# First feed-forward block in two phases with seven products for eight, and the state-space tables moved beside its second layer

## The chip, the cores and the metric

The program runs on one core of one Trainium2 chip. The metric is the device time of one execution in microseconds; before the change it was 2383.15 us, the median of three runs (2380.75 to 2388.32). TensorE multiplies a stationary block of up to 128 x 128 weights with moving columns, VectorE (DVE), ScalarE (ACT) and GpSimd (POOL) work element by element, and the queues of SyncE (SP), ACT and POOL issue DMAs.

## The reference

One layer of a hybrid decoder for 1024 prompt positions and 8 sample positions, 1032 rows of 1024 channels in all:

```
x = x + 0.5 * swiglu(rms_norm(x, g_ffn1), w1_gate, w1_up, w1_down)   # 1024 -> 2816 -> 1024
h = rms_norm(x, g_mix); proj = h @ w_in                              # u | q | k | v | gates
y_ssm  = s5_branch(u, ...)      # state-space model, 32 groups, needs tables from a, dt, b, c
y_attn = dilated attention over three windows
x = x + (gate_ssm * (y_ssm @ w_ssm_proj) + gate_attn * (y_attn @ w_attn_proj)) @ w_o
x = x + 0.5 * swiglu(rms_norm(x, g_ffn2), w2_gate, w2_up, w2_down)
swiglu(x) = (silu(x @ w_gate) * (x @ w_up)) @ w_down
```

It also returns key/value windows (mostly copies of the caches) and the final state-space states.

## The kernel before

The rows of x are transposed to channels on the partitions and split into three chunks of 344 columns (`CH`, `NCH`): `xT[c]` is 128 x 8 x 344. All products run with each operand split into a high and a low part (`ah`/`al` for x, `h`/`l` for weights: a ScalarE cast and a VectorE subtraction, `loadw` and `parts`), and three matmuls stand for one exact product. The hidden width 2816 makes 22 tiles f of 128, or 11 pairs j.

*First block, before* (`ffn`, L171): for each f, `gateup` loads a gate and an up tile (512 KB each), splits them, and makes both products for each of the three chunks, 8 x 3 matmuls each; the hidden values stay in SBUF, split (`hh`, `hl`). After every second f, `down` multiplies the pair before with its rows of `w1_down` and adds into `xT` on VectorE (L200). The last four f are one group, chunk by chunk, and after each chunk `norm` makes the operands of the next stage. `fill` calls `ssm_tables` for one of ten steps per pair: step 0 (`ssm_poles`) is a long chain of small VectorE instructions; the following ones make the state-space tables of four groups each: powers R on GpSimd (L416 to L430, doubling a length from 1 to 128, one buffer R), products on VectorE, transposes on TensorE, stores by SP.

`load_x` (L916) loads x in nine blocks, makes each row's scale by ACT and VectorE, transposes on TensorE and copies into `xT`; after blocks 2, 5 and 8 `scaled` makes the operands of a chunk.

*Second block, before and after*: in two phases. `wo_norm` (L1244) stores the chunk's x to `x_d` (a DMA by POOL), sums squares, scales `xT` in place and makes the operands: chunks 0 and 1 together are a 2 x 2 block matrix (channels halves by chunks), for which seven products stand for eight; their operands B11, B21, B22, T1 to T4 are halves of the chunks, and sums and differences of them; D0 and D1 are chunk 2, done directly. `wprep` makes the weights' sums. `ffn_up` (L1350) runs through f: products A11 B11, S2 T2, S3 T3, S1 T1, A12 B21, A22 T4, S4 B22, then chunk 2's; `second` forms what the second layer needs of the hidden values and stores it to `hs_d` by POOL. `ffn_down` (L1493) runs the pairs j in groups, product by product (P1 to P7 and `lo`, `hi` for chunk 2): `hload` fetches an operand from `hs_d` into one of four slots in turn (the first four by SP, then by POOL), `wsplit` splits the weights, `run` makes four PSUM banks and adds them into accumulators. The operand slots are memory of the first layer's operands (`slot`, `SLOT`).

The order of work: instructions are written in program order, and a planner orders each engine's queue by a simulated timeline: what comes earlier in the program goes first when it is ready, and what is ready may go ahead of what isn't. DMAs follow on the queue that issues them. `keep_in_program_order` holds the cache copies on ACT's queue (one after each weight load, `shift`) and the loads of x (`xin`).

After the first block, `mix` makes u tiles, eight state-space batches that read the tables from memory, gates, attention and the output projection.

Of the kernel before, what the change touches and what calls it, by code (L numbers as in the profile page):

```python
# [12 lines left out]
ALU = mybir.AluOpType  # L13
# [46 lines left out]
class Step:  # L60
# [49 lines left out]
    def norm(s, pool, c, z, xT, ah, al):  # L110
        nc = s.nc
        ss = pool.tile([128, CH], F32, name="ss", bufs=1)
        for k in range(KT):
            if k == 0:
                nc.scalar.activation(ss, xT[c][:, k], AF.Square)
            else:
                sq = pool.tile([128, CH], F32, name="sq", bufs=2)
                nc.scalar.activation(sq, xT[c][:, k], AF.Square)
                (nc.gpsimd if k <= PN[z] else nc.vector).tensor_add(ss, ss, sq)
        p = s.pt.tile([128, 512], F32, name="pT")  # L120
        nc.tensor.matmul(p[:, :CH], s.ones, ss, start=True, stop=True)
        s.scaled(pool, c, z, xT, ah, al, s.rsq(pool, p[:, :CH], 1.0 / D))

    def scaled(s, pool, c, z, xT, ah, al, r):
        nc = s.nc
        for k in range(KT):
            xn = pool.tile([128, CH], F32, name="xn", bufs=2 if z else XN)
            nc.vector.scalar_tensor_tensor(xn, xT[c][:, k], s.gains[:, z, k:k + 1], r, op0=ALU.mult, op1=ALU.mult)  # L128
            nc.scalar.copy(ah[c][:, k], xn)  # L129
            (nc.gpsimd if k % PL[z] == 1 else nc.vector).tensor_sub(al[c][:, k], xn, ah[c][:, k])  # L130

# [33 lines left out]

    def new_act(s):
        s.ah = [s.act.tile([128, KT, CH], F32R, name=f"ah{c}") for c in range(NCH)]
        s.al = [s.act.tile([128, KT, CH], F32R, name=f"al{c}") for c in range(NCH)]


    def ffn(s, hp, tmp, wg, wu, wd, xT, after, fill=None, lg=4):  # L171
        nc = s.nc
        H = {}

        def gateup(f):
            Wg, Wu = s.pre or (s.colw(wg, 128 * f), s.colw(wu, 128 * f))
            s.pre = None
            hh = hp.tile([128, NCH, CH], F32R, name="hh")
            hl = hp.tile([128, NCH, CH], F32R, name="hl")
            for c in range(NCH):  # L180
                pg, pu = s.dense(Wg, c), s.dense(Wu, c)
                h = tmp.tile([128, CH], F32, name="h")
                nc.scalar.activation(h, pg, AF.Silu)
                nc.vector.tensor_mul(h, h, pu)  # L184
                nc.scalar.copy(hh[:, c], h)
                nc.vector.tensor_sub(hl[:, c], h, hh[:, c])
            H[f] = hh, hl

        def down(fs):
            W = [s.loadw(wd[0][128 * f:128 * f + 128, :].rearrange("p (m q) -> p m q", q=128)) for f in fs]  # L190
            last = fs[-1] == NF - 1
            if last:
                order = [(m, c) for c in range(NCH) for m in range(KT)]
            else:
                order = [(m, c) for m in range(KT) for c in range(NCH)]
            for m, c in order:
                p = s.pm.tile([128, 512], F32, name="pm")[:, :CH]
                for i, f in enumerate(fs):
                    s.mm3(p, W[i], H[f], [(m, c)], i == 0, i == len(fs) - 1)
                nc.vector.scalar_tensor_tensor(xT[c][:, m], p, 0.5, xT[c][:, m], op0=ALU.mult, op1=ALU.add)  # L200
                if last:
                    after(c, m)

        for f in range(0, NF, 2):
            gateup(f)
            gateup(f + 1)
            if f and f < NF - 2:
                down((f - 2, f - 1))
            if fill:
                fill(f // 2)  # L210
        if lg < 4:
            down(range(NF - 4, NF - lg))
        down(range(NF - lg, NF))
# [606 lines left out]
    def run(s):  # L820
        tc, nc, i = s.tc, s.nc, s.i
        with ExitStack() as ctx:
# [49 lines left out]

            with ExitStack() as c1:
                psum(c1, 6, 2)
                xp, tmp = pool(c1, "xp"), pool(c1, "tmp", 2)
                xT = [xp.tile([128, KT, CH], F32, name=f"xT{c}") for c in range(NCH)]
                s.new_act()

                def first():
                    s.pre = s.colw(i['w1_gate'], 0), s.colw(i['w1_up'], 0)  # L880

                with ExitStack() as c_:
                    s.load_x(pool(c_, "xrp"), xT, first)
                stp = pool(c1, "stp")
                hp = pool(c1, "hp", 4)

                def after(c, m):
                    if m < KT - 1:
                        return
                    if c == 0:  # L890
                        s.new_act()
                    s.norm(tmp, c, 1, xT, s.ah, s.al)
                    nc.sync.dma_start(s.x_d[c], xT[c])

                s.ffn(hp, tmp, i['w1_gate'], i['w1_up'], i['w1_down'], xT, after, lambda n: s.ssm_tables(stp, tmp, n), LG)
# [3 lines left out]
            with ExitStack() as c6:  # L899
                hp = pool(c6, "hp2")  # L900
                c2, c01 = ExitStack(), ExitStack()
                x2, tmp, x01 = pool(c2, "x2"), pool(c2, "tmp2", 2), pool(c01, "x01")
                xT = [(x2 if c == 2 else x01).tile([128, KT, CH], F32, name=f"xT{c}") for c in range(NCH)]
                s.join(hp, xT)
                s.ep = pool(ctx, "ep", side="right")
                s.wprep(i['w2_gate'], i['w2_up'])
                s.out_norm(tmp, xT)
                c01.close()
                s.ep2 = pool(ctx, "ep2", side="right")
                s.ffn_up(pool, c6, c2, hp)  # L910
            s.wd = [pool(ctx, f"wd{z}", side="right") for z in range(2)]
            s.ffn_down(pool(ctx, "wsum", side="right"), pool(ctx, "yo"), i['w2_down'])
# [3 lines left out]
    def load_x(s, tmp, xT, first):  # L916

        nc = s.nc
        R = {}
        for b in range(9):  # L920
# [3 lines left out]
            if b == 2:  # L924
                first()
# [24 lines left out]
            if b in (2, 5, 8):  # L950
                s.scaled(tmp, b // 3, 0, xT, s.ah, s.al, R[b // 3][:, :CH])
# [33 lines left out]
    def mix(s, psum):  # L985
# [15 lines left out]
        if True:  # L1001
# [132 lines left out]
    def u_tile(s, up, m):  # L1134
        nc = s.nc
        W = s.colw(s.i['w_in'], 128 * m)
        ut, us = up.tile([128, 8, 128], F32, name="ut"), up.tile([128, 8], F32, name="us", bufs=2)
        for ch in range(NCH):
            p = s.dense(W, ch)
            nn = 43 if ch < 2 else 42  # L1140
            nc.scalar.copy(ut[:, :, 43 * ch:43 * ch + nn].rearrange("p j n -> p n j"),
                           p[:, :8 * nn].rearrange("p (n j) -> p n j", j=8))
            if ch == 2:
                nc.scalar.copy(us, p[:, 336:344])
        for g in range(8):
            dst = s.u_d[8 * m + g, 7, 0]
            nc.sync.dma_start(bass.AP(tensor=dst.tensor, offset=dst.offset, ap=[[128, 16], [-2048, 8], [1, 128]]),
                              ut[16 * g:16 * g + 16])
        nc.sync.dma_start(s.us_d[128 * m:128 * m + 128], us)
# [94 lines left out]
    def wo_norm(s, tmp, xT, c):  # L1244
# [4 lines left out]
        ss = tmp.tile([128, CH], F32, name="rs3", bufs=1)  # L1249
        for k in range(KT):  # L1250
            if k == 0:
                nc.scalar.activation(ss, xT[c][:, k], AF.Square)
            else:
                sq = tmp.tile([128, CH], F32, name="sq", bufs=2)
                nc.scalar.activation(sq, xT[c][:, k], AF.Square)
                V.tensor_add(ss, ss, sq)
            if k % 4 == 3:
                yield 1
        p = s.pt.tile([128, 512], F32, name="pT")
        nc.tensor.matmul(p[:, :CH], s.ones, ss, start=True, stop=True)  # L1260
        r = s.rsq(tmp, p[:, :CH], 1.0 / D)
        yield 1
        for k in range(KT):
# [456 lines left out]
```

## Time and profile before

| | us |
|---|---|
| median of 3 runs | 2383.15 |
| profiled execution, its own time | 2386.82 |
| its span on the core | 2384.8 |
| TensorE, VectorE, ScalarE, GpSimd busy | 2306.0, 1356.1, 786.9, 339.4 |
| mean granted TensorE clock | 0.981 |

Stages of the span: loading x to about 36 us, the first block to about 814 us, u tiles and state-space batches to about 1060 us, attention to 1380 us, output projection to about 1660 us, the second block's first layer to 2128.5 us and its second to the end. "Busy" of an engine is the time in which at least one of its instructions ran; idle time of an engine that others don't wait for costs nothing.

### The profile page before, as it was taken

The page shows a single profiled execution, that of the slowest core. Times are in us where ns is not written, and L with a number is a line of the kernel's source. Part 1 is how long each engine was busy: PE and PEld are TensorE (multiplying, and loading weights), DVE is VectorE, ACT ScalarE, POOL GpSimd, SP SyncE. Part 2 cuts the span into 40 slices and gives each one's busy share as a digit, 9 for nine tenths or more (in the row PEclk, how much of TensorE's full clock was granted, in tenths as well). Part 3 has the DMA queues.
Part 4 walks back from the last instruction along what each step waited for, and adds up shares of the span by engine and source line. Part 5 has one row for each costly group of instructions (what it writes and reads, how often), then busy time and mean ns, then how long its engine had stood idle before and what let it go on. Part 6 is the DMA issues. An engine that isn't in the chain of part 4 may idle for free.

```text
span 2384.8 us, 37168 instructions
## 1 busy us (share of the span) xinstructions
PE 2306.0 (97%) x14409; PEld 2212.2 (93%) x14409; DVE 1356.1 (57%) x2929; ACT 786.9 (33%) x1506; POOL 339.4 (14%) x929
## 2 busy tenths in 40 slices
PE   6999999999999899989999998899999999998999
PEld 6999999999999799978888897899999999998998
DVE  7655544364532834456476536488867676644574
ACT  6211112111112434455453523145433333332322
POOL 3056777000000300000000000210001000010010
PEclk8999999999999999999999998999999999998999
DMA  5333334242323377561142135766334333374553
GB/s 142 99 102 115 115 107 136 80 121 86 108 81 113 125 185 235 165 201 45 48 123 66 43 115 153 260 201 210 130 119 140 119 122 124 119 301 188 192 205 125
DMA packets 300198, 325.73 MB, mean 137 GB/s; under 512 B 38822, under 2 KB 265494, under 8 KB 297462
## 3 DMA queue, kind: packets, MB, share of 16 engines
q1 hardware_dynamic: 277478, 189.94, 26.6%
q0 software_dynamic: 18864, 85.21, 10.0%
q10 hardware_dynamic: 3680, 48.22, 6.5%
q8 instruction: 113, 1.85, 0.3%
q14 instruction: 63, 0.52, 0.1%
HBM read 243.52 MB, written 123.78 MB: 154 GB/s over the span
## 4 chain that ended last, share of the span: by engine, by line
PE 77%; DMA 8%; issue 6%; DVE 6%; ACT 2%; SPq 1%; POOL 0%; ACTq 0%; POOLq 0%; DVEq 0%
PE pm L158 44%; PE pm L1347 19%; PE pm L1544 8%; DMA r<-in_w_o_dram 2%; PE ps L671 1%; DMA rs<-g_d 1%; DMA e<-hs_d 1%; PE acc L687 1%; PE pT L680 1%; PE pn L973 1%; DVE w L1242 1%; DVE xn L128 1%; DMA xr<-in_x_prompt_dram 0%; PE pT L457 0%; DMA r<-in_w_in_dram 0%
## 5 line engine op out<-in xcount | busy, mean ns | idle before, releaser
L158 PE MATMUL pm<-ah,w 128*128 128x344 f32 x4192 | 1010.1, 324 | 14.1 <-ACT ah L129 3.8
L158 PEld LDWEIGHTS pm<-ah,w 128*128 128x128 f32 x4192 | 727.8, 189 | 31.5 <-issue 9.5
L158 PE MATMUL pm<-al,w 128*128 128x344 f32 x2384 | 722.5, 326 | 6.2 <-ACT al L1172 2.8
L158 PEld LDWEIGHTS pm<-al,w 128*128 128x128 f32 x2384 | 443.2, 190 | 17.8 <-issue 8.1
L158 PE MATMUL pm<-hh,w 128*128 128x344 f32 x1056 | 253.7, 321 | 0.0
L143 ACT CAST w<-r 128x1024 fp32r<-128x1024 f32 (+1 forms) x124 | 120.5, 978 | 369.6 <-PE pm L158 340.7
L144 DVE TENSOR_TENSOR w<-r,w 128x1024 fp32r<-128x1024 f32 (+1 forms) x124 | 142.3, 1149 | 154.1 <-ACT w L143 141.6
L1241 ACT CAST w<-r 128x1024 fp32r<-128x1024 f32 (+1 forms) x130 | 125.6, 968 | 295.0 <-PE pm L1347 171.5
L158 PEld LDWEIGHTS pm<-hh,w 128*128 128x128 f32 x1056 | 183.6, 188 | 0.4
L1242 DVE TENSOR_TENSOR w<-r,w 128x1024 fp32r<-128x1024 f32 (+1 forms) x130 | 145.3, 1120 | 67.5 <-ACT w L1241 67.4
L1347 PE MATMUL pm<-ah,w 128*128 128x344 f32 x1056 | 182.7, 321 | 1.0 <-ACT ah L1241 1.0
L1347 PE MATMUL pm<-e,w 128*128 128x344 f32 x1056 | 179.2, 321 | 1.2 <-DVE w L1242 1.0
L200 DVE SCALAR_TENSOR_TENSOR xT<-pm,xT 128x344 f32<-128x344 f32 x240 | 121.8, 514 | 93.3 <-PE pm L158 93.2
L1347 PEld LDWEIGHTS pm<-ah,w 128*128 128x128 f32 x1056 | 170.2, 189 | 1.6 <-ACT ah L1241 1.2
L1347 PEld LDWEIGHTS pm<-e,w 128*128 128x128 f32 x1056 | 169.1, 188 | 1.7 <-DVE w L1242 1.3
L158 PE MATMUL pm<-hl,w 128*128 128x344 f32 x528 | 169.5, 321 | 0.0
L184 DVE TENSOR_TENSOR h<-h,pm 128x344 f32<-128x344 f32 x66 | 33.7, 511 | 190.4 <-PE pm L158 190.3
L1347 PE MATMUL pm<-al,w 128*128 128x344 f32 x792 | 137.7, 323 | 2.5 <-ACT p L1427 2.5
L1347 PEld LDWEIGHTS pm<-al,w 128*128 128x128 f32 x792 | 128.2, 189 | 3.1 <-ACT p L1427 2.8
L1544 PE MATMUL pm<-e,x 128*128 128x344 f32 x636 | 105.6, 320 | 0.9 <-ACT x L1241 0.9
L1544 PEld LDWEIGHTS pm<-e,x 128*128 128x128 f32 x636 | 100.8, 188 | 1.2 <-ACT x L1241 1.2
L158 PEld LDWEIGHTS pm<-hl,w 128*128 128x128 f32 x528 | 99.1, 188 | 0.2
(429 smaller groups left out, 2866.8 us busy)
## 6 DMA issues: line engine op xcount, KB each, us to landing
out_dram<-in_cache_kv_w_dram ACTq DMA_DIRECT2D x64, 512.0 KB
hs_d<-hs POOLq DMA_DIRECT2D x44, 688.0 KB, 4.5
r<-in_w_gate_dram SPq DMA_DIRECT2D x44, 512.0 KB
r<-in_w_up_dram SPq DMA_DIRECT2D x44, 512.0 KB
r<-in_w_in_dram SPq DMA_DIRECT2D x38, 512.0 KB
r<-in_w_down_dram SPq DMA_DIRECT2D x36, 512.0 KB
e<-hs_d POOLq DMA_DIRECT2D x11, 1376.0 KB, 6.9
r<-in_w_o_dram SPq DMA_DIRECT2D x24, 512.0 KB
```

The costliest lines, as they stand in the source:

```text
L128: nc.vector.scalar_tensor_tensor(xn, xT[c][:, k], s.gains[:, z, k:k + 1], r, op0=ALU.mult, op1=ALU.mult)
L143: nc.scalar.copy(h[:, :k], raw[:, :k])
L144: nc.vector.tensor_sub(l[:, :k], raw[:, :k], h[:, :k])
L158: nc.tensor.matmul(p, w[:, kw], a[:, ka], start=first and i == 0, stop=last and i == n - 1)
L184: nc.vector.tensor_mul(h, h, pu)
L200: nc.vector.scalar_tensor_tensor(xT[c][:, m], p, 0.5, xT[c][:, m], op0=ALU.mult, op1=ALU.add)
L671: nc.tensor.matmul(p[h][:, :nk], qT[hs, s.block(g, b)], kT[hs, ks], start=True, stop=True)
L680: nc.tensor.transpose(pt[:, h, i], sm[:, h, 128 * i:128 * i + 128], s.ident)
L1241: s.nc.scalar.copy(hi, x)
L1242: s.nc.vector.tensor_sub(lo, x, hi)
L1347: nc.tensor.matmul(p, W[w][:, k], B[:, a, k], start=first and k == 0 and z == 0, stop=k == n - 1 and z == 2, skip_group_check=True)
L1544: nc.tensor.matmul(p[m], W[wz][:, m], t[:, jj, az], start=e == 0 and z == 0, stop=e == n - 1 and z == 2, skip_group_check=True)
```

## The change

The first block takes the second block's form. `norm`, `scaled`, `new_act` and `ffn` go; `up` (a new function around `ffn_up`) and `ffn_down` serve both blocks, with z = 0 for the first and 1 for the second.

- `load_x` scales by `wo_norm` with a given row scale r, so each chunk is stored to `x_d`, scaled in place and turned into the operands; the weights of the first tile are prepared in between; chunk 2 is left to `ffn_up` (`norm2`).
- `ffn_down` has one order of products for both blocks and two sets of slots. In the first block it runs 11 pairs in groups of 3, 3, 3 and 2 (the second block keeps 4, 4, 3), accumulates into the next `xT`, calls `ssm_tables` after every third run (1, 4, ... 28 of 36), and `normed` makes the mixing stage's operands chunk by chunk, by `wo_norm` with `put`.
- `u_tiles` does two u tiles together, chunk by chunk, instead of one after the other.
- The sums of squares are added on VectorE alone.

```diff
+            def up(z, front):
+                with ExitStack() as c6:
+                    hp = pool(c6, "hp2")
...
+                    front(hp, tmp, xT, ce)
+                    c01.close()
+                    s.ep2 = pool(ce, "ep2", side="right")
+                    s.ffn_up(pool, c6, c2, hp)
+                return ce
...
-                s.ffn(hp, tmp, i['w1_gate'], i['w1_up'], i['w1_down'], xT, after, lambda n: s.ssm_tables(stp, tmp, n), LG)
+                up(0, front1).close()
+                with ExitStack() as c7:
+                    s.ffn_down(0, pool, c7, i['w1_down'])
...
             if b in (2, 5, 8):
-                s.scaled(tmp, b // 3, 0, xT, s.ah, s.al, R[b // 3][:, :CH])
+                r = tmp2.tile([128, CH], F32, name=f"rs{b // 3}", bufs=1)
+                nc.scalar.copy(r, R[b // 3][:, :CH])
+                N.append(s.wo_norm(tmp2, xT, b // 3, 0, r))
+            if b == 2:
+                for _ in N[0]:
+                    pass
+                for _ in range(2):
+                    next(s.prep[0])
+        s.ep = loaded()
+        for _ in N[1]:
+            next(s.prep[0], None)
+        s.norm2 = N[2]
...
-                        for m in range(4):
-                            s.u_tile(up, m)
+                        for m in (0, 2):
+                            s.u_tiles(up, (m, m + 1))
...
+        if z:
+            GR = [list(range(0, 4)), list(range(4, 8)), list(range(8, NP))]
...
+            HS = ('al1', 'e0', 'e1', 'al2')
...
+        else:
+            GR = [list(range(0, 3)), list(range(3, 6)), list(range(6, 9)), list(range(9, NP))]
...
+            HS = ('al1', 'al0', 'ah2', 'al2')
...
+            tmp, stp = pool(ctx, "tmp", 2), pool(ctx, "stp")
...
-            t = s.slot(('e0', 'e1', 'al2', 'e2')[hn[0] % 4], [128, 4, 2, CH], F32R)
+            t = s.slot(HS[LAST[name] if last else hn[0] % 4], [128, 4, 2, CH], F32R)
...
+            pn[0] += 1
+            if not z and pn[0] % 3 == 1 and pn[0] < 30:
+                s.ssm_tables(stp, tmp, pn[0] // 3)
...
+        def normed(c):
+            if z:
+                return
+            s.ah[c], s.al[c] = (s.act.tile([128, KT, CH], F32R, name=n) for n in
+                                ((HS[3], 'ah1'), ('ah0', HS[2]), (HS[0], HS[1]))[c])
...
+            for _ in s.wo_norm(tmp, xT, c, 1, put=put):
+                pass
...
+            run([(W, t1, e) for e, W in enumerate(A11)], 'P1')
+            run(prod(X, 'P5'), 'P5')
...
+            run(W, 'P6')
...
+            run(W, 'P7')
...
+            if not last:
+                xin('lo')
+                run(prod(X, 'P3'), 'P3')
+                A12 = ops(1, half0, "wb")
+                xin('P4')
+                run(prod(A12, 'P2', None), 'P2')
+                td = hload('d1'), hload('d2')
+                xin('hi')
+                run(both(A11, A12, td), 'lo')
+                A22 = ops(1, half1, "wb")
+                run(prod(A22, 'P4', None), 'P4')
+                xin('x')
+                A21 = ops(0, half1, "wa")
+                run(both(A21, A22, td), 'hi')
+                continue
...
+            run(W, 'P4')
+            out(0, 1, 'P4')
+            A12 = ops(1, half0, "wc")
+            run(prod(A12, 'P2', None), 'P2')
+            out(0, 0, 'P2')
+            W = prod(X, 'P3')
+            td = hload('d1'), hload('d2')
...
+            run(W, 'P3')
+            normed(0)
+            out(1, 0, 'P3')
...
+            run(both(A11, A12, td), 'lo')
+            normed(1)
+            out(2, 0, 'lo')
+            if z:
+                run(both(A21, A22, td), 'hi', lambda m: m % 2 and out(2, 1, 'hi', (m - 1, m)))
+            else:
+                run(both(A21, A22, td), 'hi')
+                normed(2)
```

In the last group of either block, `LAST` gives the slots: P1, P5, P6, P7 the four in turn, P4, P2, P3 the first three again, d1 and d2 the first two.

## Rows read from the trace of the kernel before

**Rows 1.** the page, parts 1 and 2: busy us by engine; VectorE's busy tenths

```profile
PE 2306.0 (97%) x14409; PEld 2212.2 (93%) x14409; DVE 1356.1 (57%) x2929; ACT 786.9 (33%) x1506; POOL 339.4 (14%) x929
...
DVE  7655544364532834456476536488867676644574
```

**Rows 2.** stretches: from:to, us, busy us (instructions) of PE PEld DVE ACT POOL, clock, DMA, GB/s

```profile
45.00:785.00 740.00, 740.00 (x4686) 727.86 (x4685) 359.87 (x966) 137.01 (x232) 220.06 (x732) 1.00 0.34 104
142.00:445.00 303.00, 303.00 (x1918) 297.16 (x1917) 146.42 (x344) 51.27 (x84) 196.25 (x675) 1.00 0.37 113
783.00:815.00 32.00, 26.09 (x159) 25.04 (x159) 28.30 (x47) 16.66 (x33) 15.58 (x15) 0.98 0.11 45
815.00:840.00 25.00, 19.30 (x74) 15.74 (x74) 23.20 (x44) 11.90 (x22) 3.85 (x10) 0.76 0.67 217
1650.00:1690.00 40.00, 35.39 (x208) 33.95 (x208) 37.10 (x55) 25.44 (x30) 0.53 (x1) 0.96 0.32 100
1690.00:2110.00 420.00, 420.00 (x2651) 419.63 (x2650) 285.28 (x418) 151.43 (x213) 34.09 (x50) 1.00 0.39 128
2128.00:2156.00 28.00, 17.96 (x113) 17.67 (x113) 6.57 (x12) 4.82 (x10) 2.81 (x4) 0.86 1.02 410
2156.00:2220.00 64.00, 63.06 (x385) 62.78 (x385) 36.25 (x61) 20.79 (x39) 4.50 (x6) 0.96 0.52 190
2220.00:2320.00 100.00, 100.00 (x639) 99.96 (x639) 62.12 (x111) 25.10 (x45) 8.23 (x11) 1.00 0.50 176
```

**Rows 3.** timeline of TensorE, end of the second block's first layer: start, us

```profile
2113.28 2.06 PE L1347 MATMUL pm<-ah,w 128*128 128x344 f32 x12
2115.17 2.06 PE L1347 MATMUL pm<-al,w 128*128 128x344 f32 x12
```

**Rows 4.** timeline of TensorE and the SP queue at the second block's joint

```profile
2155.62 3.81 PE L1544 MATMUL pm<-e,w 128*128 128x344 f32 x12 [10.04 <-DMA e<-hs_d]
...
2159.23 3.17 PE L1544 MATMUL pm<-al,w 128*128 128x344 f32 x12
...
2128.64 0.38 SPq L1516 DMA_DIRECT2D e<-hs_d  x1
```

**Rows 5.** DMA issues: count, KB each, median us from issue to landing

```profile
x_d<-xT POOLq DMA_DIRECT2D x3, 1376.0 KB, 9.6
...
e<-hs_d POOLq DMA_DIRECT2D x6, 1032.0 KB, 5.4
```

**Rows 6.** timeline: the first block's start, and VectorE before the second block

```profile
26.30 1.52 DVE L128 SCALAR_TENSOR_TENSOR xn<-xT,gains,pm 128x344 f32<-128x344 f32 x3
...
36.08 0.63 PE L158 MATMUL pm<-ah,w 128*128 128x344 f32 x1
...
1646.99 3.99 DVE L1264 SCALAR_TENSOR_TENSOR xT<-xT,gains,rs 128x344 f32<-128x344 f32 x8
...
1651.33 1.58 DVE L1280 TENSOR_TENSOR xT<-xT,xT 128x1376 f32<-128x1376 f32 x1
```

**Rows 7.** VectorE in 45 to 785 us by line: count | busy, mean ns | idle before

```profile
L200 DVE SCALAR_TENSOR_TENSOR xT<-pm,xT 128x344 f32<-128x344 f32 x228 | 115.8, 515 | 93.3 <-PE pm L158 93.2
L144 DVE TENSOR_TENSOR w<-r,w 128x1024 fp32r<-128x1024 f32 x62 | 76.3, 1234 | 59.8 <-ACT w L143 59.6
L186 DVE TENSOR_TENSOR hl<-h,hh 128x344 fp32r<-128x344 f32 x66 | 34.8, 527 | 17.1 <-ACT hh L185 16.9
L184 DVE TENSOR_TENSOR h<-h,pm 128x344 f32<-128x344 f32 x66 | 33.7, 511 | 190.4 <-PE pm L158 190.3
```

**Rows 8.** chain of waits in 280 to 440 us, about one table's transposes: start, us

```profile
361.97 0.32 PE pT L457 x2
...
364.04 51.98 PE pm L158 x330
```

**Rows 9.** one line's and one tensor's instructions: count, ns min/median/max, first and last start

```profile
L423 POOL TENSOR_TENSOR q<-R,PO x112: 185/239/1377, 111.6 to 410.9; 128x2 f32<-128x2 f32 x16, 128x4 f32<-128x4 f32 x16, 128x8 f32<-128x8 f32 x16, 128x16 f32<-128x16 f32 x16
...
L1516 POOL DMA_DIRECT2D e<-hs_d x17: 741/748/781, 2136.5 to 2331.5; - x17
```

More of the change, by code (lines that the diff above doesn't have):

```diff
@@ L108, in rsq @@
         return e
[L110 to L130, printed above, removed]
     def loadw(s, src, k=KT, d=0):
@@ L164, in dense @@
         return p[:, :CH]
[L166 to L213, printed above, removed]
     def pexp(s, out, x, t):
@@ L871, in run, with front1, front2 @@
             s.wq = pool(ctx, "wq")
+            def up(z, front):
+                with ExitStack() as c6:
+                    hp = pool(c6, "hp2")
+                    c2, c01 = ExitStack(), ExitStack()
+                    x2, tmp, x01 = pool(c2, "x2"), pool(c2, "tmp2", 2), pool(c01, "x01")
+                    xT = [(x2 if c == 2 else x01).tile([128, KT, CH], F32, name=f"xT{c}") for c in range(NCH)]
+                    ce = ctx if z else ExitStack()
+                    front(hp, tmp, xT, ce)
[3 more added lines that the diff above has]
+                return ce
+            def front1(hp, tmp, xT, ce):
+                s.wprep(i['w1_gate'], i['w1_up'])
+                with ExitStack() as c_:
+                    cp = ExitStack()
+                    s.load_x(pool(cp, "xrp", side="right"), tmp, xT, lambda: (cp.close(), pool(ce, "ep", side="right"))[1])
+            def front2(hp, tmp, xT, ce):
+                s.join(hp, xT)
+                s.ep = pool(ce, "ep", side="right")
+                s.wprep(i['w2_gate'], i['w2_up'])
+                s.out_norm(tmp, xT)
             with ExitStack() as c1:
+                s.wq2 = pool(c1, "wq2")
                 psum(c1, 6, 2)
[L875 to L893, printed above, removed]
-                s.ffn(hp, tmp, i['w1_gate'], i['w1_up'], i['w1_down'], xT, after, lambda n: s.ssm_tables(stp, tmp, n), LG)
+                up(0, front1).close()
+                with ExitStack() as c7:
+                    s.ffn_down(0, pool, c7, i['w1_down'])
             s.mix(psum)
@@ L898, in run, with load_x @@
             psum(ctx, 6, 2)
[L899 to L912, printed above, removed]
+            up(1, front2)
+            s.ffn_down(1, pool, ctx, i['w2_down'])
             while copies:
                 shift()
-    def load_x(s, tmp, xT, first):
+    def load_x(s, tmp, tmp2, xT, loaded):
         nc = s.nc
-        R = {}
+        R, N = {}, []
         for b in range(9):
@@ L1596, in rows, with ops, prod, both @@
                     s.shift()
-                    raw[e][z] = x
+                    raw[e][q] = x
+            def ops(q, h, nm):
+                return [wsplit(r[q][:, h], nm, e) for e, r in enumerate(raw)]
+            def prod(X, name, nm="ws"):
+                t = hload(name)
+                return [((wsplit(x, nm, e) if nm else x), t, e) for e, x in enumerate(X)]
+            def both(X, Y, t):
+                return [(W[q], t[q], e) for e, W in enumerate(zip(X, Y)) for q in range(2)]
@@ L1599, in ffn_down @@
             rows(0)
-            t1 = hload('P1', js)
+            t1 = hload('P1')
             rows(1)
-            def ops(z, h, nm):
-                return [wsplit(r[z][:, h], nm, e) for e, r in enumerate(raw)]
-            def two(X, Y, t):
-                return [(W[z], t[z], e) for e, W in enumerate(zip(X, Y)) for z in range(2)]
-            def S(nm, e, f):
-                x = wd.tile([128, 512], F32, name=nm)
-                f(x, raw[e])
-                return x
-            def sums():
-                return [S(f"S{e}", e, lambda x, r: V.tensor_add(x, r[0][:, half1], r[1][:, half1])) for e in range(len(js))]
@@ L1654, in ffn_down @@
-            A1 = ops(0, half0, "wa")
-            X = sums()
-            run(prod(A1, 'P1', None), acc('P1', g))
-            run(prod(X, 'P5'), acc('P5', g))
+            A11 = ops(0, half0, "wa")
+            X = []
+            for e, r in enumerate(raw):
+                X.append(sp.tile([128, 512], F32, name=f"S{e}"))
+                V.tensor_add(X[e], r[0][:, half1], r[1][:, half1])
+            run([(W, t1, e) for e, W in enumerate(A11)], 'P1')
+            run(prod(X, 'P5'), 'P5')
             for r, x in zip(raw, X):
@@ L1659, in ffn_down @@
                 V.tensor_sub(x, x, r[0][:, half0])
+            xin('P3')
             W = prod(X, 'P6')
[L1661 to L1670 removed]
@@ L1671, in ffn_down @@
-            u12('P4', 'P7')
-            u12('P5', 'P7')
-            out(1, 1, A['P5'])
-            run(prod(A22, 'P4', None), acc('P4', g))
-            out(0, 1, A['P4'])
+            if last:
+                u12('P3', 'P5')
+                u12('P5', 'x')
+            run(W, 'P6')
+            for r in raw:
+                V.tensor_sub(r[0][:, half0], r[0][:, half0], r[0][:, half1])
+            xin('P2')
+            W = prod([r[0][:, half0] for r in raw], 'P7')
+            if last:
+                u12('P6', 'P1')
+                u12('P3', 'P6')
+                u12('P2', 'P1')
@@ L1688, in ffn_down @@
-            out(2, 0, A['lo'])
-            def ev(m, p):
-                half(A['hi'][:, m], p)
-                if m % 2:
-                    out(2, 1, A['hi'], (m - 1, m))
-            run(two(A21, A22, td), ev, 1)
+            if not last:
[13 more added lines that the diff above has]
+                continue
```

223 lines of the change are left out of this document (102 added, 121 removed).

## The prediction

> **What bounds the kernel now.** I read the page's first two parts before anything else: TensorE is busy for 97% of a span of 2384.8 us, VectorE for 57%, and VectorE's digit row never falls to zero [rows 1]. Next the table of stretches, because an average says nothing about one stage. The reader is to see three things in it: in the first feed-forward block (45 to 785 us) TensorE is busy in every microsecond at the full granted clock, with VectorE at half load and GpSimd at 30%; the second block's first layer (1690 to 2110 us) is as dense with VectorE at 68%; and only around the joints (783 to 840, 1650 to 1690, 2128 to 2156 us) does TensorE lose time [rows 2]. So inside the blocks the bound is the number of matmuls times their spacing, and at the joints it is what VectorE or a DMA delivers late. Spacing: twelve matmuls of 344 columns start 1.89 us after the twelve before them, 0.158 us each [rows 3]. The profiled execution took 2386.82 us, 3.67 above the median of the three timed runs (2383.15); the sum is made against 2386.82 and the result shifted by that.
>
> **The change part by part.**
>
> *Fewer products.* Layer one of the first block does 22 x 2 x 3 x 8 x 3 = 3168 matmuls; with seven products for the two large chunks and the third chunk done directly it does 22 x (28 + 16) x 3 = 2904. Layer two does 1584, and then 11 x (84 + 48) = 1452. That is 264 + 132 = 396 fewer, times 0.158 = **-62.5 us**. All of it comes if TensorE stays as dense as now, nothing if another engine sets the pace; the parts below say how much is given back. The products' sums go to memory and back (55 stores, 36 loads); the second block carries the same traffic at a DMA share of 0.39 and 0.50 without a loss [rows 2], so I cost it at nothing.
>
> *The second block's joint.* Both blocks now share one second layer with another order of products: P1, P5, P6, P7 first, the pair d1, d2 after six. Today d2 goes into the slot of an operand that the first layer's last matmuls read, so its load is issued at 2128.64 and TensorE stands for 10.04 us until 2155.62; the next two dozen matmuls take 3.61 and about 3.0 us for 1.89 each [rows 4]. In the new order the first load goes into a slot free some 20 us before the layer ends, the pair is needed six products (45 us) after the start instead of two (15 us), and x is fetched piece by piece. I take 10.0 + 2.8 = **-12.8 us** (bounds -14, and 0 if the first rows' splits are late next). In the last group d2 now waits for P2, one product ahead of its use: 5.4 us for the landing [rows 5] against 5.7 us of P3, so 1 to 2 us at most, left to the range. The first block's new joint is the same code; I give it 0, bounds 0 and +5.
>
> *The start.* Today dense matmuls start at 36.08 us, with the first chunk [rows 6]. Then, only the first 12 products need that chunk alone; the next need sums of chunks 0 and 1. Chunk 1 is ready for scaling at 26.3 us [rows 6]. New is that its store to memory must finish before it is scaled in place: 9.6 us for such a store [rows 5], while the scalings wait on VectorE with everything of this chunk behind them. Then eight scalings, 4.0 us, and six differences and remainders of 1.58 us up to the first new operand [rows 6]: 26.3 + 9.6 + 4.0 + 9.5 = 49 us, three more operands at 1.58 each behind it, and chunk 2's scaling and two operands (7.2 us of VectorE) before the third tile may go on, some 5 us more. The 12 early products give 1.9 back. Net **+15 us** (bounds +8, if the store starts early, and +25, if weights and stores collide). Nothing hides it: there is nothing else to multiply.
>
> *The state-space tables beside the second layer.* They lay beside 700 us of matmuls and come beside some 230. VectorE's load: in 2156 to 2320 us it is busy 98.4 of 164 us [rows 2], 0.60, so 138 us for 1452 matmuls. Four groups instead of three make 36 product runs of 27: 9 x 4 additions of 0.515 = +18. The tables: 359.9 us busy in 45 to 785 [rows 2] less 115.8 + 76.3 + 34.8 + 33.7 of the block's own [rows 7], less some 10 of scaling left over from the load, is 89. Together 245 us. TensorE's load: 229 us, and the tables' transposes (361.97 to 364.04 us, 2.07 for each of eight [rows 8]) make 246. Two engines are full at once. What that costs I read from three stretches: 1690 to 2110 us with VectorE at 68% lost nothing; 1650 to 1690 with 93% recorded 208 matmuls, 32.9 us of work, and lost 7 (18%); 783 to 840 with 51.5 of 57 us recorded 233, 36.8 us, and lost 20 (35%) [rows 2]. I take 13% of 246, **+32 us**: near the second, which also mixes weight splits with operands, and a little below it, since spare slots let splits run ahead. Bounds +5 and +86 (the third, a tail with a chain in it).
>
> *GpSimd.* Each table is a chain there: 16 batches from 111.6 to 410.9 us, 19 us each [rows 9]. It outlasts the new second layer and runs into the mixing stage, whose state-space batches use the tables one after the other. But 32 of the 36 operand loads are issued by GpSimd too, 0.75 us each [rows 9], in one order with the chain; each waits for a slot, and what stands behind a waiting load is the chain and the loads after it. Four slots give three products (17 us) of lead. If the loads are slipped into the chain's gaps (GpSimd was idle 107 of 303 us in 142 to 445 [rows 2]) the cost is nothing; if they stand behind whole batches, each is late. I take **+5**, bounds 0 and +118 (a rival below). The tables' 48 stores move with them on the SP queue, between 22 row loads whose next need is a whole group (62 us) off: nothing.
>
> The Trainium skill, "SBUF — State Buffer", section "Who interferes with whom", says that a VectorE instruction with two SBUF inputs and a GpSimd one that reads SBUF keep each other out for a whole instruction. The row: the chain's first multiplication has a median of 239 ns and a longest of 1377 [rows 9], so the trace agrees that a few are held up; the loads' issues stay within 741 to 781 ns beside a VectorE at 60% [rows 9, 2].
>
> *The tail into the mixing stage.* Today it loses the 20 us just named. Then the norms of chunks 1 and 2 are each 4.0 + 7 x 0.51 + some 2.7 + 3.2 = 13.5 us of VectorE, and with two sets of additions and the next weights 33 us from the end of the run "lo"; TensorE has the 48 matmuls of "hi" and the paired u tiles' 96 (instead of 48) before it needs chunk 2, 22.8 us: 11 lost instead of 20, of which I take **-6** (bounds -12, and +10 because GpSimd no longer adds the squares).
>
> Sum: -62.5 - 12.8 + 15 + 32 + 5 - 6 = **-29.3**, so 2357.5 for this execution and 2354 beside the median. I predict 2355 us.
>
> **The rivals.** (1) *The tables interleave without loss*: +5 for +32, 0 for GpSimd, sum -61: 2322 beside the median. For it: TensorE didn't idle once in 45 to 785 us with the same tables [rows 2]; against it: VectorE had half its time free there. (2) *GpSimd becomes the bound*: slower. If the operand loads stand behind table batches in its queue, the layer can't end before the chain does: some 40 us for the poles (today the chain begins 66 us into the block), 300 of chain, 24 of issues, 364 instead of 246: +118 in place of the +37, sum +52, 2435. It decides once about half of the 16 batches stand ahead of the last load; with +66 the gain is gone. For it: the tables come earlier in the program than the loads of the runs behind them; against it: the chain's gaps. (3) *The gain is eaten at the joints*: start +25, layer +50, GpSimd 0, tail +5: sum +5 or a little below, 2376 to 2388. (4) *The port lock as the skill's page has it*: with VectorE full, the larger chain instructions (some 12 of a batch) each take the longest row, 1 us more: 16 x 12 x 1 = 190 us of GpSimd; where loads stand behind them it ends at (2)'s time or above.
>
> **How the numbers follow.** Forecast 0.45; (1) 0.21; (2), with (4) at 0.04 in it, 0.22; (3) 0.12. A difference under 0.3% (7 us) can't be told from none here. Faster is the forecast and (1), 0.66; no change is (3), 0.12; slower is (2), 0.22. The forecast's own range, with a layer loss of 8 to 20% and the start's bounds, is 2335 to 2376. The range for 8 in 10 goes from just under (1), 2318, to 20 us short of (2), 2415.
>
> **What would show it.** TensorE's matmul count falls by 396. At the second block's joint the wait for hs_d is gone and the clock stays at 1.00. The dense stretch begins at 49 to 56 us. In the first block's second layer VectorE is over 90% busy and the layer lasts 270 to 285 us; under 250 (1) is right, and over 310 with TensorE waiting for loads that GpSimd issued, (2). The u tiles begin with less than 15 us lost. I am wrong if the first layer itself isn't dense, or if the mixing stage waits for tables.

## The result and the profile after

The changed kernel takes 2487.1 us (median of 4 runs, 2484.4 to 2490.2) against 2385.0 beside it: ratio 1.043, interval 1.041 to 1.045. It is slower by 102 us; I had predicted 2355. The landmarks of the two traces, in us from the span's start, put the loss into stages (the last column is how much longer the stage is):

| stage | before | after | longer by |
|---|---|---|---|
| to the first dense product | 36.1 | 56.8 | 20.7 |
| from there to the first u tile | 775.6 | 810.3 | 34.7 |
| u tiles and state-space batches, to the first gated (glu) product | 201.9 | 238.2 | 36.3 |
| from there to the second block's second layer | 1114.9 | 1111.2 | -3.7 |
| that layer, to the end | 256.3 | 268.4 | 12.1 |
| span | 2384.8 | 2484.9 | 100.1 |

The second row holds the 62.5 us of saved products, so 97 us were lost there. The page's first two parts, to be read beside [rows 1]:

```profile
PE 2273.3 (91%) x14013; PEld 2175.2 (88%) x14013; DVE 1555.5 (63%) x3217; ACT 888.5 (36%) x1613; POOL 433.9 (17%) x986
...
PE   4999999978985677998999999899999999989989
...
DVE  7766666668884753455557544568866666645554
...
POOL 1000000003387777300000000120000000010000
PEclk6999999989997888999999999999999999999999
```

TensorE does 396 matmuls fewer, as reckoned. Its row sinks from slice 9 to 16 (497 to 994 us), and its clock with it; GpSimd's is up from slice 10 to 17, while VectorE's falls from 8 to 3. Stretches of the changed kernel, with the columns of [rows 2]:

```profile
57.00:517.00 460.00, 458.75 (x2887) 458.10 (x2888) 311.01 (x457) 169.78 (x236) 34.80 (x51) 0.99 0.52 177
517.00:867.00 350.00, 269.25 (x1571) 253.53 (x1569) 252.45 (x827) 74.71 (x137) 188.44 (x416) 0.89 0.61 206
867.00:941.00 74.00, 54.34 (x291) 52.50 (x292) 34.60 (x52) 25.51 (x40) 59.17 (x164) 0.83 0.39 117
941.00:1105.00 164.00, 145.11 (x925) 142.77 (x925) 71.65 (x146) 64.57 (x132) 61.02 (x213) 0.94 0.64 186
```

The first layer is dense and takes its 460 us for 2904 matmuls. The second has the VectorE work I had added up (252 us, I had 245), but lasts 350 us instead of 283: VectorE is 72% busy, not full. What TensorE waited for in 515 to 960 us (total, times, longest), and when the 16 batches of powers were stored:

```profile
PE pm L1518 <- DMA al<-hs_d: 44.0, 4, 26.9
PE pm L136 <- ACT al L1181: 14.4, 2, 8.2
PE pT L306 <- DVE PO L240: 9.7, 1, 9.7
PE pm L136 <- ACT ah L1181: 8.0, 1, 8.0
```

```profile
L359 POOL DMA_DIRECT2D r_d<-R x16: 597/598/617, 666.7 to 1019.1; - x16
```

The chain of powers [rows 9] ends at 1019 us, 501 us after the layer began. The longest wait, on the timeline of all engines:

```profile
762.13 10.02 POOL L352 TENSOR_TENSOR q<-R,PO 128x4 f32<-128x4 f32 x1
762.33 0.17 DVE L369 TENSOR_TENSOR b<-b,b 128x32 f32<-128x32 f32 x1
762.43 0.67 DVE L1182 TENSOR_TENSOR x<-S,x 128x512 fp32r<-128x512 f32 x1
...
769.25 0.39 PE L386 MATMUL pT<-sq,b 128*16 128x128 f32 x2
...
771.41 0.67 DVE L1182 TENSOR_TENSOR x<-S,x 128x512 fp32r<-128x512 f32 x1
...
788.39 0.18 POOL L345 COPY R<-PO 128x2 f32<-128x2 f32 x1 [1.81 <-DMA r_d<-R]
...
791.93 0.74 POOL L1490 DMA_DIRECT2D al<-hs_d  x1
...
796.53 5.78 PE L1518 MATMUL pm<-al,w 128*128 128x344 f32 x24 [26.89 <-DMA al<-hs_d]
```

TensorE ran out of work at 769.6. The operand that it wants sits in GpSimd's order behind a whole batch and the start of the next; its load is issued at 791.93, without any wait of its own. One instruction of that batch, 4 elements wide, took 10.02 us while VectorE ran some twenty instructions without a gap. Seven of the 16 batches are stored ahead of the last load, which is issued at 840.42.

### The profile page after: what moved, and what is told of

It is laid out like the page before. It is cut to its first block, busy times and chain, and to the rows that moved or that the text cites. A ratio compares the mean times of both kernels' runs of the same rounds, so it can differ in the third digit from the quotient of the medians.

```text
span 2484.9 us, 37155 instructions
## 1 busy us (share of the span) xinstructions
PE 2273.3 (91%) x14013; PEld 2175.2 (88%) x14013; DVE 1555.5 (63%) x3217; ACT 888.5 (36%) x1613; POOL 433.9 (17%) x986
## 4 chain that ended last, share of the span: by engine, by line
PE 50%; issue 24%; POOL 11%; DMA 10%; DVE 3%; ACT 1%; SPq 1%; ACTq 0%; POOLq 0%; DVEq 0%
PE pm L1292 18%; PE pm L136 14%; PE pm L1518 11%; DMA r_d<-R 2%; POOL q L352 2%; PE ps L600 2%; POOL R L354 2%; POOL hs_d L1320 1%; POOL R L357 1%; POOL q L353 1%; POOL q L355 1%; POOL q L356 1%; PE acc L616 1%; PE pT L609 1%; DMA r<-in_w_down_dram 1%
## 5 line engine op out<-in xcount | busy, mean ns | idle before, releaser
L1181 ACT CAST w<-r 128x1024 fp32r<-128x1024 f32 (+1 forms) x253 | 239.8, 949 | 549.6 <-PE pm L1292 351.6
L1292 PE MATMUL pm<-ah,w 128*128 128x344 f32 x2112 | 364.3, 321 | 2.0 <-ACT ah L1181 1.5
L1292 PE MATMUL pm<-e,w 128*128 128x344 f32 x2112 | 357.4, 320 | 4.0 <-ACT e L1181 2.4
L136 PEld LDWEIGHTS pm<-al,w 128*128 128x128 f32 x1936 | 324.5, 192 | 34.4 <-ACT al L1181 14.9
L1292 PEld LDWEIGHTS pm<-ah,w 128*128 128x128 f32 x2112 | 340.0, 189 | 2.5 <-ACT ah L1181 1.7
L1292 PEld LDWEIGHTS pm<-e,w 128*128 128x128 f32 x2112 | 337.1, 188 | 5.0 <-ACT e L1181 2.8
L1182 DVE TENSOR_TENSOR w<-r,w 128x1024 fp32r<-128x1024 f32 (+1 forms) x253 | 277.5, 1098 | 87.0 <-ACT w L1181 86.5
L136 PE MATMUL pm<-ah,w 128*128 128x344 f32 x1472 | 318.7, 331 | 13.6 <-ACT ah L1181 8.0
L136 PEld LDWEIGHTS pm<-ah,w 128*128 128x128 f32 x1472 | 250.5, 193 | 25.0 <-ACT ah L1181 8.3
L1292 PEld LDWEIGHTS pm<-al,w 128*128 128x128 f32 x1584 | 256.6, 189 | 0.7 <-ACT p L1372 0.5
L1518 PEld LDWEIGHTS pm<-al,w 128*128 128x128 f32 x1260 | 207.3, 195 | 44.1 <-issue 36.0
L1320 POOL DMA_DIRECT2D hs_d<-hs x110 | 75.0, 682 | 885.4 <-DVE hs L1182 849.1
L122 DVE TENSOR_TENSOR w<-r,w 128x1024 fp32r<-128x1024 f32 (+1 forms) x58 | 60.4, 1042 | 92.8 <-ACT w L121 89.4
L1518 PE MATMUL pm<-al,x 128*128 128x344 f32 x564 | 98.6, 321 | 0.0
L1518 PEld LDWEIGHTS pm<-al,x 128*128 128x128 f32 x564 | 90.4, 189 | 0.5 <-DVE x L1182 0.2
L121 ACT CAST w<-r 128x1024 fp32r<-128x1024 f32 (+1 forms) x58 | 52.1, 899 | 88.5 <-PE pm L136 44.6
L1518 PE MATMUL pm<-e,x 128*128 128x344 f32 x384 | 66.8, 329 | 14.7 <-ACT x L1181 14.7
```

The costliest lines, as they stand in the source:

```text
L121: nc.scalar.copy(h[:, :k], raw[:, :k])
L122: nc.vector.tensor_sub(l[:, :k], raw[:, :k], h[:, :k])
L136: nc.tensor.matmul(p, w[:, kw], a[:, ka], start=first and i == 0, stop=last and i == n - 1)
L1181: s.nc.scalar.copy(hi, x)
L1182: s.nc.vector.tensor_sub(lo, x, hi)
L1292: nc.tensor.matmul(p, W[w][:, k], B[:, a, k], start=first and k == 0 and z == 0, stop=k == n - 1 and z == 2, skip_group_check=True)
```

## Experiments

The same kernel once more, to see how far it moves:

> The changed kernel once more, beside the others of this call: how far its time moves between calls. In the run with the second block's old order, the first block's instructions stand in the same order on every engine, yet its u tiles began 17.6 us earlier than in the changed kernel's profile. If the changed kernel stays at 2484 to 2490, that comes from the kernels; at 2465 to 2480 it is the first block's own spread, and differences of that size in the first block tell nothing.

2480.9 us, 2465.5 to 2490.9; the profile looks like the first one (u tiles at 865.9 us). The kernel spreads by 1% by itself, the kernel before, run beside it, by 0.6%: a difference under some 20 us from 2484 is not read below unless a stage of the trace shows it.

**Taking the chain away.**

```
-            ... (two copies and the 42 products and sums of the seven doublings)
+            P.memset(R, 0.0)
```

> The powers R of the tables are left out: one GpSimd instruction writes zeros into R, which is stored as before; VectorE's, TensorE's and DMAs' part of the tables stays. Theories A and C (GpSimd is the cause, by order or by length): second layer near 250 us instead of 349 and no wait for tables in the mixing stage, time 2350 to 2400. Theory B (VectorE): the layer stays above 320 us and the time above 2450.

2417.2 us (ratio to the kernel before 1.014, interval 1.012 to 1.015): 70 us less than the first measurement of the changed kernel, 64 less than the second. The u tiles begin at 817.6 instead of 867.1 and the glu stage at 1034.6 instead of 1105.3. So GpSimd's chain is a cause, and B's 2450 is not reached. But A and C hold only in part: the time is 17 us above their range, and the layer takes 300 us, not 250. Now without any of the 16 batches (the poles stay):

> All 16 table batches are left out (zeros by GpSimd are stored in their place); the poles and the inputs stay. Against the run without the power chain this takes away some 85 us of VectorE's work, 64 small products and transposes on TensorE. Theory B: another 40 to 90 us less than without the chain. Theories A and C: 5 to 25 us less than without the chain (16 us of it TensorE's own transposes and products). Time 2330 to 2385; what is then left above 2322 is start and joints.

2401.7 us, 15.4 less again, about what I had counted for the tables' own products on TensorE (8 times 2.07). B has fallen: VectorE's share of the tables costs next to nothing. But the time is above the forecast range too and stays 18 above the kernel before. The second layer's stretch in these two runs (without powers, without tables):

```profile
517.00:817.00 300.00, 267.05 (x1575) 248.44 (x1573) 248.06 (x827) 74.66 (x137) 44.49 (x69) 0.93 0.74 247
```

```profile
516.00:806.00 290.00, 242.46 (x1475) 237.70 (x1474) 197.64 (x523) 69.16 (x122) 58.04 (x118) 0.94 0.76 256
```

VectorE is busy for 83% of the first stretch and 68% of the second, and the layer hardly changes: even without the batches, 1452 products (229 us at 0.158) take 290.

**Order or length.** What stands behind the chain on GpSimd was taken from it step by step:

```
-            q = nc.sync if hn[0] < 4 else nc.gpsimd
+            q = nc.sync if hn[0] < 4 or not z else nc.gpsimd
```

> The first block's 32 later operand loads are issued by the SP queue instead of GpSimd; nothing else changes. Theory A (order): TensorE's 47 us of waits for al and ah from hs_d in the second layer, and the slow clock behind them, come from loads that stand behind table instructions in GpSimd's order. Then these waits fall under 15 us, GpSimd no longer stands 61 us for slots so that its power chain ends near 940 us instead of 1020, and the time falls by 50 to 90 us, to 2400 to 2435. Theory B (VectorE is full): the loads were late because everything else was late; TensorE then waits for split weights and accumulations instead, and the time stays within 15 us of 2487. Theory C (length): the layer gets faster but the mixing stage waits longer for the last tables, gain under 30 us.

2465.2 us. The 44 us of waits for operands fell to 2.7, but the chain still ended at 983.2, not near 940, and the u tiles began at 845.1, after 47.0 us of waiting for their operand. I took that for the store of x, which stood behind the chain too:

```
-        nc.gpsimd.dma_start(s.x_d[c], xT[c])
+        (nc.sync if z == 1 else nc.gpsimd).dma_start(s.x_d[c], xT[c])
```

> The first block's operand loads and also the stores of x before the mixing stage's norms go by SP, so that GpSimd has only the table chain left. Theory A with C (order, then length): in the run with the loads alone on SP, the mixing operands waited 47 us because the store of x stood behind the chain on GpSimd; now the u tiles begin near 805 us instead of 845, but the state-space batches still wait for the last table, which is stored at 970 to 985 us: time 2445 to 2465. If the chain's end does not bound it, 2420 to 2435.

2470.0 us, and the wait is still there: the store was not the cause. Timeline of all engines in this run:

```profile
833.66 0.34 POOL L510 IOTA aip<- 128x256 int32 x1
834.04 0.33 DVE L511 CAST aif<-aip 128x256 f32<-128x256 int32 x1 [45.05 <-POOL aip L510]
...
848.73 0.94 PE L136 MATMUL pm<-al,w 128*128 128x344 f32 x2 [52.77 <-ACT al L1181]
```

An index pattern for the attention masks, 0.34 us of GpSimd that only the attention stage needs, came behind the chain; VectorE, which takes its instructions in order, stood for it 45 us, and the norm behind VectorE. So:

```
+        s.m12 = s.cst.tile([128, 256], F32, name="m12")
+        nc.gpsimd.iota(s.m12.bitcast(I32), ...)        # in consts, at the start
```

> As the run with loads and x stores by SP, and the index pattern for the masks is made by GpSimd at the program's start instead of behind the tables. Order alone: the u tiles begin near 805 us instead of 849 and the time falls by 35 to 45 us, to 2425 to 2435. Length: the u tiles begin near 805 us, but the batches then wait for the last tables (stored at 970 to 985 us), the glu stage begins at 1070 to 1085 us as before, and the time is 2455 to 2470, no or little gain.

2462.0 us, with the u tiles at 804.4: they come 63 us sooner than in the changed kernel, the glu stage, at 1080.4, only 25. TensorE's waits in 860 to 1090 us, and the chain's stores:

```profile
PE pT L435 <- POOL q L358: 37.8, 1, 37.8
...
L361 POOL DMA_DIRECT2D r_d<-R x16: 599/599/614, 655.6 to 980.8; - x16
```

Length, then: the state-space batches need the last table, and 38 of the 63 us are given back there. The chain itself starts late: its first batch is stored at 655.6, 139 us into the layer, though no load stands in GpSimd's queue any more. Up to then GpSimd waited 82 us for the poles from VectorE (`PO`):

```profile
POOL q L354 <- DVE PO L242: 39.5, 5, 17.0
POOL R L347 <- DVE PO L242: 35.0, 1, 35.0
POOL q L355 <- DVE PO L242: 7.8, 3, 4.7
```

The chain's end bounds the time also without the cache copies that ACT issues:

```
-                    s.shift()
+                    if z:
+                        s.shift()
```

> The cache copies that ACT issues after each row load are left out of the first block's second layer (they are issued later, after other loads). In the trace ACT stands 9 to 12 us in such issues at 539 to 557 us, with PSUM evictions behind them. Theory: that wait goes and with it 10 to 25 us, 2462 to 2477, if TensorE isn't caught by the poles at once; no gain (2480 to 2490) if the transposes that wait for the poles end last there anyway.

2480.5 us. The layer was 56 us shorter (u tiles at 811.1), but the last powers were stored at 1053.8 and the glu stage began at 1086.0; the time is within the spread.

**The chain where GpSimd is idle.** Poles and powers were moved into the first layer:

```
+            if not zz and f == 2:
...
+                pg.append(s.ssm_poles(s.rp))      # a step at each nxt()
...
+            if not zz and f > 5:
+                s.ssm_chain(2 * (f - 6))
```

> The poles and all power chains R are made beside the first block's first layer (GpSimd is busy 35 of 475 us there, VectorE 326), one batch per f from f = 6, the poles in steps over f = 2 to 5; the rest of the tables stays in the second layer. Two small tiles of the first layer get one buffer instead of two to make room. Theory A (GpSimd's chain in the second layer is the largest loss): about as fast as the run that left the chain out, 2405 to 2425, and a little less still, 2395, if the poles at the joint cost time too. Against it: the first layer is no longer dense, because VectorE and GpSimd hold each other up; then over 2440.

2455.5 us. The first layer is no longer dense, as in the case against it, and lasts to 577.5, so that the u tiles come at 860.6; but it isn't VectorE and GpSimd that hold each other up. ACT's largest wait but that for TensorE in 100 to 577 us, and TensorE's largest in the program:

```profile
ACT hs L1194 <- DMA hs_d<-hs: 96.6, 20, 13.2
```

```profile
PE pm L1305 <- DVE v L1406: 43.7, 7, 7.9
```

The stores of hidden values, issued by GpSimd, stood behind the chain: the same fault, one layer earlier. With them on SP, and the second block's order of before:

```
-                nc.gpsimd.dma_start(s.hs_d[i:i + n, j]...
+                (nc.gpsimd if zz else nc.sync).dma_start(s.hs_d[i:i + n, j]...
```

> Chain and poles beside the first layer as before, the first layer's stores of hidden values issued by SP instead of GpSimd, and the second block's first two groups in the old order. In the run with the chain in the first layer, that layer took 521 us instead of 461: its stores stood behind the chain on GpSimd (96.6 us of ACT waiting for them), the same mechanism as in the second layer. Theory A: the layer is dense again within 15 us, and the time 2365 to 2395. Against it: a VectorE at 75% beside a busy GpSimd is what slows the layer; then 2410 to 2430.

2373.2 us (0.995, 0.994 to 0.997), 114 and 108 less than the two measurements of the changed kernel and 0.5% faster than the kernel before. Some 22 of that are the second block's order (below). The glu stage begins at 1015.9, 89 us sooner than in the changed kernel: for chain and poles together, which no run tells apart. Its stretches:

```profile
57.00:517.00 460.00, 458.79 (x2893) 458.25 (x2894) 347.30 (x658) 169.93 (x238) 268.02 (x693) 1.00 0.55 185
517.00:801.00 284.00, 256.16 (x1564) 241.65 (x1562) 226.62 (x623) 73.77 (x135) 38.42 (x64) 0.96 0.74 247
801.00:850.00 49.00, 30.45 (x140) 28.60 (x141) 31.20 (x50) 19.14 (x30) 1.22 (x7) 0.75 0.33 104
```

GpSimd does 268 us in the first layer beside a VectorE that is 75% busy, and that layer loses nothing. Two tries at the rest:

> As the run with early chain, stores by SP and old order, and no cache copies from ACT in the first block's second layer. That edit alone shortened the layer by 56 us (u tiles at 811 instead of 867 us) but the time by 7, which the theory puts down to the chain's end. With the chain gone from there it should bring 10 to 30 us: 2345 to 2375. If it brings under 5, the copies were not in the way.

2378.0 us (2368.6 to 2383.8): the u tiles come 5 us sooner, at 796.1, and the time shows no gain; the copies were not in the way any more.

> As the run with the chain beside the first layer, hidden stores by SP and the second block's old order, with the chain begun one f sooner (f = 5), so that the last powers are stored some 20 us before the first layer ends. There VectorE stood 13.5 us for that store (the tables' tiles lie over R's memory) and TensorE 12.7 us behind it. If that is the cause: 2355 to 2366. If another wait (PSUM evictions behind the cache copies on ACT) takes its place: 2368 to 2376.

2370.6 us (0.994, 0.993 to 0.995). The last powers were stored at 531.3 us, as before the edit (531.1): the chain begins at 167.7 instead of 166.6, since VectorE's steps for the poles end no sooner, and VectorE still stood 10.1 us for that store. The edit did not do what it said, so what the wait costs was not tested.

**The second block's joint.**

```
-        LAST = {'P1': 0, 'P5': 1, ...}
+        LAST = {'P1': 2, 'P5': 1, 'P6': 3, 'P7': 0, ...} if z else {'P1': 3, 'P5': 2, ...}
```

> The last group's products take other operand slots, in both blocks: P1 goes to a slot that is free a product earlier, not to that of d1 or d2, which the run hi of the group before still reads. Theory: the second block's wait of 6.9 us (with the slow clock behind it some 8) goes, and the first block's of 26.9 us at 796 us falls if it is the slot, and stays if it is the load's place behind the table chain. Slot in both: -25 to -40, 2447 to 2462; slot in the second block alone: -6 to -10, about 2479.

2463.0 us. The second block's 6.9 us are gone and its second layer takes 258.7 instead of 268.4. The first block's part (u tiles at 845.9) can't be told from its spread.

```
+            if z and not last:      # P1, P2, lo, hi, P4, P5, P6, P7, P3
...
```

> The second block's first two groups run their products in the order of the kernel before (P1, P2, lo, hi, P4, P5, P6, P7, P3); the first block and the operand slots stay as changed. Theory: the 14.7 us at the joint come from P5 in second place, whose weights are sums that wait for memory under the last stores of hidden values; in the old order the sums are needed 50 us later and d2 now has a slot that is free early. Both waits (14.7 and 6.9 us) go with the slow clock behind them: -20 to -28, 2459 to 2467. If the joint moves to another wait instead: under -10.

2453.0 us; the layer takes 246.4 us, 22 less, and both waits are gone. The rest of the difference lies ahead of it: the u tiles come at 849.5, in a first block with the same instructions, and I put that down to its spread. Timeline of the changed kernel at this joint, against [rows 4]:

```profile
2216.47 7.68 PE L1518 MATMUL pm<-al,w 128*128 128x344 f32 x48
...
2226.50 1.28 POOL L1320 DMA_DIRECT2D hs_d<-hs  x2 [1.27 <-DVE hs L1182]
2237.45 0.69 DVE L1601 TENSOR_TENSOR S<-r,r 128x512 f32<-128x512 f32 x1 [10.83 <-DMA hs_d<-hs]
...
2238.85 3.52 PE L1518 MATMUL pm<-e,x 128*128 128x344 f32 x11 [14.71 <-ACT x L1181]
```

P5 now comes second; its weights are sums S, and S lies over memory that the last stores of hidden values still read. The slots alone, on the kernel before:

```
-        ... ('al1', 'lo', 'hi') ...      ('e0', 'e1', 'al2', 'e2')[hn[0] % 4]
+        ... ('e2', 'lo', 'hi') ...       ('al1', 'e0', 'e1', 'al2')[hn[0] % 4]
```

> The kernel before, with only the second block's operand slots changed as the change does it: the loads turn through al1, e0, e1, al2 instead of e0, e1, al2, e2, and the sums lo and hi lie in e2. Order of products as before. Theory: this alone takes away the 10.0 us of waiting for d2 and the slow clock behind it, -12.8 as predicted: 2369 to 2374. Rival: x for lo and hi, now loaded into the slot of an operand that is read last, is late: no change or slower, 2380 to 2390.

2370.4 us (0.9948, 0.993 to 0.996), inside the forecast; the interval is 9 to 16 us of gain, so that a hit to 1 us is luck. The layer takes 243.9 us. TensorE's longest wait from 2000 us to the end:

```profile
PE pm L1544 <- ACT x L1241: 1.4, 1, 1.4
```

These two edited lines are as good as anything built on the change.

## Why the prediction was wrong

*Fewer products* was right: 396 fewer at 0.158, and the first layer gave its 41.7 us.

*GpSimd, +5*, is the step that failed. It was rival (2): I had named the mechanism and its condition, and given it 0.22 because of the gaps in the chain. Those gaps were fewer than I read: of my 107 idle us, 29 lie behind the chain's last store (415.1). The runs put the chain at 64 to 70 us. Taking all that is urgent out of its queue gave back only 19 to 25 (2462.0 us), so that its length is the larger part.

The rival's picture was not right either. Its layer could not end before the chain; in fact the layer ended at 867.1, 104 us over my 246 (the rival had 118), with eight of the 16 batches still to be stored. The chain ended 501 us into it, not 364, and so the batches behind it, which I had charged with nothing, stood for its end too (36 us of the table above). Two things made it that late. The first batch was stored after 149 us, where I had some 60 (40 for the poles, 19 for the batch); without loads in the queue it was 139. Then a batch took 23.5 us against 18.3 before, and of these its own products and sums took 16.1 against 12.6. That is the sum of six lines, of which one is shown, after (15 batches) and before (16 batches):

```profile
L352 POOL TENSOR_TENSOR q<-R,PO 128x2 f32<-128x2 f32 (+6 forms) x105 | 49.9, 475 | 6.7
```

```profile
L423 POOL TENSOR_TENSOR q<-R,PO 128x2 f32<-128x2 f32 (+6 forms) x112 | 34.0, 303 | 19.2 <-DVE PO L311 12.0
```

The wait for the store of the single buffer R did not grow (36 us, 43 before). "I am wrong if the mixing stage waits for tables" was the right sign to watch.

*The tables beside the second layer, +32*: the sum of VectorE's work was right, its price wrong. Leaving out the rest of the tables gives 15 us. A VectorE at 72% was no bound. In the 2373.2 us run the layer takes 284 us, within my 270 to 285; since it takes 290 without the batches, that is luck.

*The second block's joint, -12.8*: the mechanism and size were right for the slots (the run on the kernel before), the term wrong for the change, since its new order put another wait there, 14.7 us, and P1 of the last group into the slot of a d2 still read, 6.9: +12.1. My bound of 0 did not hold a wait on memory freed by stores.

*The start, +15*: 20.7, but not by the way I had reckoned. The row at 26.30 in [rows 6] is the first chunk's scaling; the second chunk's began at 35.91, which my 26.3 and 9.6 for the store add up to by luck. In the changed kernel the second chunk's store was issued at 27.58 and wasn't what its scaling waited for: that began at 42.15, when its row scale had been copied (41.67), which waited on VectorE behind the first chunk's scaling and operands. Timelines, before (first line) and after:

```profile
35.91 2.02 DVE L128 SCALAR_TENSOR_TENSOR xn<-xT,gains,pm 128x344 f32<-128x344 f32 x4
```

```profile
27.58 0.56 POOL L1188 DMA_DIRECT2D x_d<-xT  x1 [12.80 <-ACT rn L101]
...
32.12 3.98 DVE L1205 SCALAR_TENSOR_TENSOR xT<-xT,gains,rs 128x344 f32<-128x344 f32 x8
...
41.67 0.45 ACT L879 COPY rs<-pm 128x344 f32<-128x344 f32 x1
...
42.15 1.07 DVE L1205 SCALAR_TENSOR_TENSOR xT<-xT,gains,rs 128x344 f32<-128x344 f32 x2
...
56.80 0.65 PE L1292 MATMUL pm<-e,w 128*128 128x344 f32 x1 [1.77 <-ACT e L1181]
```

*The tail, -6*: where no chain is in the way (the 2373.2 us run) the stage from the first u tile to glu takes 214.8 us, 13 more than before, with 140 matmuls in 49 us at a clock of 0.75. TensorE stands there for the norms' operands (6.8 and 8.3 us), which no run took away.

*Rival (1)*, no loss: no run comes near its 2322. In the 2373.2 us run 62.5 us are gained, 20 lost at the start, 32 in the second layer and 13 behind it, so that the first block gains nothing and the 12 us are those of the second block's joint. What the 32 are made of is only partly shown: 12.7 are a wait for the chain's last store, with a clock of 0.66 in 535 to 560 us, and 6.4 a wait for the first norm's operands at the layer's end.

*Rival (4)*: the hold-ups are there (10.02 us in the fence above), and some dearer than the 1 us each I took from [rows 9], but few: a batch's products and sums grew by 3.4 us, not 12. No run separates them from the chain's length.

## What to carry to other kernels

A long chain on an engine that is "off the critical path" is safe only as long as nothing else on that engine's queue is urgent: list every load, store and stray instruction that shares its order before moving it beside shorter work, and count when its result is needed. Work moved from 740 us of cover to 250 needs a cover longer than its own chain, not only free busy time. And try the parts of a large change alone: here two lines of it held all of the gain that any run reached.

## What the runs showed of the hardware

A GpSimd multiplication with two inputs from SBUF, 0.19 us as a rule, took 10.02 us beside an unbroken row of VectorE instructions. The Trainium skill, "SBUF — State Buffer", section "Who interferes with whom", has the two block each other for an instruction; here it was a row of some twenty, most with two SBUF inputs. That the row held it is read from the two standing side by side; no run took the row away. Issuing can hold up ACT: in the run without tables five cache copies of 512 KB took ACT's queue 12.50 us; ACT did nothing else for 13.80, and TensorE waited 12.1 for the PSUM evictions behind them.
